# Hybrid decoder layer: weight loads ahead of the last store, five open steps, another order of the down products

## The chip, the cores and the metric

The kernel runs on one core of a Trainium2 chip. The metric is the device time of one execution in microseconds. Five engines with queues of their own work side by side: TensorE (PE, matmuls; its weight loads are listed apart as PEld), VectorE (DVE), ScalarE (ACT), GpSimd (POOL) and SyncE (SP), which here issues all DMAs. Each works through its own queue in order.

## The reference, cut to what matters

One layer over 1024 tokens of width 1024. An input projection feeds two attention groups; their outputs are mixed by `w_out`. Then, in f32:

```
x   = layer_norm(ALPHA * x + mix, ln1_g, ln1_b)
gu  = x @ w_up                                    # 1024 -> 2 * 2816
ffn = (silu(gu[:, :2816]) * gu[:, 2816:]) @ w_down
x   = layer_norm(ALPHA * x + ffn, ln2_g, ln2_b)
ple = sigmoid(x @ w_ple_gate) * (p @ w_ple)
x   = layer_norm(ALPHA * x + ple, ln3_g, ln3_b)
```

The change touches the end of the first norm, both matmuls of the feed-forward part, and the second norm.

## The kernel before

Every f32 operand of a matmul is split in two parts whose sum is the operand: a high part (ACT or POOL, `hi`) and the rest (`lo`, DVE: the operand less its high part). `mm3` then issues three matmuls: high by high, high by low, low by high. So each block of 128x128 by 512 costs three matmuls, and each operand costs a split on two engines before PE can use it. A `hi` and its `lo` of one 128x1024 operand are called a split below. The third matmul of a block needs the `lo` of the weights.

The feed-forward part multiplies two-by-two blocks with seven products in place of eight (sums and differences of blocks stand in for the eighth). Its tiles:

- **Up stage** (`u_prod`, `u_evac`): 22 steps i of 128 hidden columns. Each has seven products (i, n), n = 1 to 7, of 12 matmuls each. Products 1 and 2 need the gate weights of the step as they are ("g", L1025 or L1031, split by `u_split(i, "g")`). 5, 6, 7 and 3 need sums of weight blocks (`u_sum`, four POOL operations of 128x512, then splits "s12" and "s34"); 4 needs the split "u". On the other side stand seven operands made of the transposed first-norm output: "11" and "21" from token blocks 0 to 3; "22", "t1" to "t4" need also blocks 4 to 7 (`tr_x1` transposes a block, `t_sums` subtracts, `put` splits into place; one `put` is two small operations of 128x256 on ACT and two on DVE).
- **The order of the up products** is a list `seq`, written out before the loop: first (i,1), (i,2) of the first SKEW steps (the open steps), which need no sums and only "11" and "21"; then step by step the others. `at_pos(k, ...)` hangs fetches, sums, splits and `put`s on places k of that list. The Python order is the order in each engine's queue.
- **The end of the first norm**: for token block tb, `out_proj(tb)` multiplies by `w_out`, ACT scales, `x1_done(tb)` multiplies and adds the norm's weights on DVE (L914, L918) and stores the block to DRAM (L1190). SP's queue is in order, so what stands behind a store waits until the store's data is there.
- **Down stage**: 77 units (n, m), seven products of 11 pairs m each, in the order `ORDER` (L1225). A unit loads two 128x512 pieces into one of four staging buffers `kk` (`d_load`, four units ahead), splits them (`d_split`, two units ahead) and multiplies into four PSUM banks B. Products 1, 6, 5, 3 go to banks XB, products 2, 7, 4 to YB; 1, 2 and 7 start from fresh banks, the others go on adding in theirs. After each product DVE adds the banks to the residual `acc` (L1346 to L1352).
- **Beside the down units** the table `more` hangs work on places k: every fourth unit a weight of the last stage (`pT`, `wple`, `wgate`) is loaded and split (POOL `hi`, L107, then DVE `lo`), and from unit `base` on the second norm of blocks 0 to 3 is made in steps (`ln2_step`: statistics on DVE and POOL, scaling on ACT, weights on DVE).

Tiles named `b` come from a pool of 43 buffers of 128x1024, tiles named `h` from 12 of 128x512; PSUM has eight banks. A load into a buffer waits until its last reader is done. `hd` and `td` are DRAM tiles: hidden blocks and sums of down weights, written during the up stage and read by the down units.

Of the kernel before, what the change touches and what calls it, by code (L numbers as in the profile page):

```python
# [11 lines left out]
OP = mybir.AluOpType  # L12
# [5 lines left out]
NB = T // 128  # L18
# [16 lines left out]
SLOTS = 43  # L35
HALVES = 12
DPAIRS = 11
SKEW = 4
PVLAG = 2
CDMA = 1  # L40
LATK = (1, 1)
# [26 lines left out]
def body(tc, sb, dr, A, out, dbg, stop):  # L68
# [13 lines left out]
    def hslot(dt=F32, n=512):  # L82
        return sb.tile([128, 512], dt, name="h", tag="h", bufs=HALVES)[:, :n]
# [915 lines left out]
    def t_sums(tb):  # L999

        b11, b21, b12, b22 = TX[tb - 4, "11"], TX[tb - 4, "21"], TX.pop((tb, "12")), TX[tb, "22"]
        t2 = hslot()
        dve.tensor_sub(b11, b12, b11)
        dve.tensor_sub(t2, b22, b11)
        pool.tensor_tensor(b12, b22, b12, op=OP.subtract)
        pool.tensor_tensor(b21, b21, t2, op=OP.subtract)
        TX.update({(tb, "t1"): b11, (tb, "t2"): t2, (tb, "t3"): b12, (tb, "t4"): b21})

    def put(tb, nm):
# [149 lines left out]
    for i in range(NF):  # L1159
        s12, s34 = min(pos[i, 5], pos[i, 6]), min(pos[i, 7], pos[i, 3])  # L1160
        first = min(s12, s34)
        if i >= SKEW:
            at_pos(pos[i, 1] - 2, u_split, i, "g")
        at_pos(first - 6, u_sum, i, 0)
        at_pos(first - 5, u_sum, i, 1)
        at_pos(first - 4, u_split, i, "u")
        at_pos(s34 - 2, u_split, i, "s34")
        at_pos(s12 - 2, u_split, i, "s12")
        if i < SKEW:
            at_pos(max(first - 9, 0), u_fetch, i)  # L1170
        else:
            at_pos(min(pos[i, 1] - 2, first - 6) - 5, u_fetch, i)
        if i % 2:
            m = i // 2
            at_pos(pos[i, 4] + 2, h_sums, m)
            k = min(pos[i, 4] + 1, len(seq) - 36 + 2 * m)
            at_pos(k - 5, d_fetch, m)
            at_pos(k, d_sums, m)
    for k, nm, tbs in ((0, "t2", (6,)), (2, "t3", (4, 5)), (4, "t2", (7,)), (4, "t3", (6, 7)), (5, "t1", (4, 5, 6, 7)),
                       (7, "22", (4, 5, 6, 7)), (9, "t4", (4, 5, 6, 7))):  # L1180
        for tb in tbs:
            at_pos(k, put, tb, nm)

# [11 lines left out]
    for tb in range(NB):  # L1195
        if tb + 2 < NB:
            out_load(tb + 2)
        if tb + 1 < NB:
            out_split(tb + 1)
        if tb in (6, 7):  # L1200
            g_fetch(tb - 6)
        if tb:
            x1_done(tb - 1)
        if tb == 7:
            u_split(0, "g")
        nrm = out_proj(tb)
        if tb:
            tr_x1(tb - 1)
        act.activation(acc[tb], acc[tb], AF.Identity, scale=nrm[0], bias=nrm[1])
        if 1 <= tb <= 4:  # L1210
            put(tb - 1, "11")
            put(tb - 1, "21")
        elif tb:
            t_sums(tb - 1)
    WO = None
    put(4, "t2")
    put(5, "t2")
    if stop == 3:
# [3 lines left out]
        return  # L1222


    ORDER = (1, 2, 6, 7, 5, 3, 4)  # L1225
    units = [(n, m) for n in ORDER for m in range(DPAIRS)]
    RW, UN = {}, {}

# [18 lines left out]
    for k, (i, n) in enumerate(seq):  # L1247
        u_prod(i, n)
        if last:
            u_evac(*last)  # L1250
        if k == 0:
            u_split(1, "g")
            x1_done(NB - 1)
        elif k == 2:
            tr_x1(NB - 1)
            t_sums(NB - 1)
        if k in (1, 3):
            u_split(k // 2 + 2, "g")
        if k in (0, 2):
            g_fetch(k // 2 + 2)  # L1260
        jobs(k)
        last = i, n
        if len(seq) - 6 <= k < len(seq) - 2:
            d_load(k - len(seq) + 6)
    u_evac(*last)
    d_split(0)
    d_split(1)
    h_sums(DPAIRS - 1)
    for k in sorted(todo):
        todo[k] = [x for x in todo[k] if x[0] is not h_sums]  # L1270
# [23 lines left out]

    more = {}
    for n, it in enumerate(range(tail, len(items))):
        more[24 + 4 * n] = [(split, it + 1)]
    base = 6 * DPAIRS
    NR = {}

    def ln2_step(tb, what):
# [10 lines left out]
            norm_b(acc[tb], ln2, "d")  # L1312
    for tb in range(4):
        for what, d in ((0, 0), (1, 2), (2, 3)):
            more.setdefault(base + 2 * tb + d, []).append((ln2_step, tb, what))
    XB, YB = {}, {}
    for k, (n, m) in enumerate(units):
        if m == 0:
# [13 lines left out]
        if k in (2, 13):  # L1332
            for tb in range(k // 11 * 4, k // 11 * 4 + 4):
                acc[tb] = slot(n=D)
                nc.sync.dma_start(acc[tb], x1d[tb])
        if k == 5 * DPAIRS:
            ln2 = load_ln(2)
        for fn, *args in more.pop(k, []):
            fn(*args)
        if m == DPAIRS - 1:  # L1340
            lft, rgt = slice(0, 512), slice(512, D)
            for b in range(4):
                x, y = acc[b], acc[4 + b]
                if n in (1, 6, 5, 3):
                    o = {1: x[:, lft], 6: y[:, lft], 5: y[:, rgt], 3: x[:, rgt]}[n]
                    dve.scalar_tensor_tensor(o, o, ALPHA, B[b], op0=OP.mult, op1=OP.add)  # L1346
                elif n != 7:
                    o = {2: x[:, lft], 4: y[:, lft]}[n]
                    dve.tensor_add(o, o, B[b])
            if n == 5:  # L1350
                for b in range(4):
                    dve.tensor_add(acc[4 + b][:, rgt], acc[4 + b][:, rgt], YB[b])  # L1352
            if n == 3:
                XB = None
# [136 lines left out]
```

## Time and profile before

| | before |
|---|---|
| median of 3 runs | 1488.2 us (1487.64 to 1489.09) |
| the profiled execution | 1483.0 us, span 1481.2 us |
| mean granted clock of TensorE | 0.986 |
| PE busy | 1416.6 us (96%) |
| DVE, ACT, POOL busy | 1008.2, 710.0, 588.1 us |
| DMA | 159.33 MB, mean 108 GB/s |

The runs are timed without the profiler, the profiled execution is one more. Busy is the time in which an engine has an instruction under way; matmuls overlap, so a busy PE is not PE at its peak. Start times in rows count from the start of the span. A number in brackets behind a row of the timeline is the time for which the engine was idle before it, with the instruction that ended this.

### The profile page before, as it was taken

The numbers are of one execution on the slowest core, as the hardware profiler recorded it, in microseconds if no ns is written. First come the engines' busy times: TensorE is split into PE (matmuls) and PEld (weight loads), VectorE is DVE, ScalarE is ACT, GpSimd is POOL, SyncE is SP. The second block draws the span as 40 slices with busy tenths as digits, with TensorE's granted clock in tenths as the row PEclk, the third lists the DMA queues.
The fourth block names the chain that finished last, engine by engine and source line by source line (L and its number), as shares of the span: only waits on it lengthen the run. The fifth ranks groups of instructions, "written<-read, shape, count | busy, mean of one in ns | idle before, by whom it ended". The sixth has DMA issues, their size and how long they took to land. (4 is left out here: it accounts for less than half of the span.)

```text
span 1481.2 us, 20524 instructions
## 1 busy us (share of the span) xinstructions
PE 1416.6 (96%) x7082; PEld 1179.7 (80%) x7082; DVE 1008.2 (68%) x1921; ACT 710.0 (48%) x1447; POOL 588.1 (40%) x572
## 2 busy tenths in 40 slices
PE   8999999999989999998799999999998999998997
PEld 8987878888778887886588888888877888776886
DVE  5367599999988898676855555555543555558775
ACT  3323499888888886333523333333332433333221
POOL 1321255644533347013466666666671000012331
PEclk9999899999999999999899999999999999999999
DMA  7031000000000023223155444444636766761001
GB/s 271 15 100 51 26 1 23 1 1 15 2 15 1 1 67 133 72 99 114 56 189 176 153 152 151 146 158 157 219 137 241 275 235 220 238 211 63 29 29 57
DMA packets 66344, 159.33 MB, mean 108 GB/s; under 512 B 8000, under 2 KB 8640, under 8 KB 66240
## 3 DMA queue, kind: packets, MB, share of 16 engines
q1 hardware_dynamic: 66240, 158.02, 30.9%
q8 instruction: 56, 0.92, 0.3%
q14 instruction: 48, 0.39, 0.1%
HBM read 117.88 MB, written 40.11 MB: 107 GB/s over the span
## 5 line engine op out<-in xcount | busy, mean ns | idle before, releaser
L122 PE MATMUL p<-b 128*128 128x512 f32 (+3 forms) x1524 | 585.8, 384 | 20.7 <-ACT b L105 11.7
L123 PE MATMUL p<-b 128*128 128x512 f32 (+3 forms) x1524 | 583.8, 383 | 12.4 <-DVE b L111 12.4
L124 PE MATMUL p<-b 128*128 128x512 f32 (+3 forms) x1524 | 584.1, 383 | 5.2 <-DVE b L111 4.8
L111 DVE TENSOR_TENSOR b<-b 128x1024 fp32r<-128x1024 f32 (+4 forms) x162 | 205.8, 1289 | 239.3 <-ACT b L105 136.6
L122 PEld LDWEIGHTS p<-b 128*128 128x128 f32 x1524 | 288.6, 189 | 76.6 <-ACT b L105 13.1
L123 PEld LDWEIGHTS p<-b 128*128 128x128 f32 x1524 | 288.7, 189 | 69.8 <-DVE b L111 18.5
L124 PEld LDWEIGHTS p<-b 128*128 128x128 f32 x1524 | 288.0, 189 | 65.0 <-DVE b L111 12.1
L111 DVE TENSOR_TENSOR h<-p,h 128x512 fp32r<-128x512 f32 (+1 forms) x244 | 148.8, 628 | 11.6 <-ACT h L105 10.2
L107 POOL TENSOR_SCALAR b<-b 128x1024 fp32r<-128x1024 f32 (+3 forms) x45 | 48.4, 1081 | 254.2 <-DMA b<-in_pT 77.5
L532 ACT ACTIVATE b<-b,st 128x640 f32<-128x640 f32 (+7 forms) x192 | 142.8, 744 | 9.3 <-DVE st L481 7.0
L481 DVE CUSTOM_DVE_ANT_0 b<-s,b 128x640 f32<-128x640 f32 (+7 forms) x192 | 137.5, 716 | 10.2 <-PE s L486 6.8
L105 ACT ACTIVATE h<-p 128x512 fp32r<-128x512 f32 (+1 forms) x244 | 131.9, 551 | 25.3 <-PE p L591 22.0
L105 ACT ACTIVATE b<-kk 128x1024 fp32r<-128x1024 f32 x77 | 81.0, 1059 | 123.9 <-DMA kk<-in_wdown 56.4
L591 PE MATMUL p<-ident,b 128*128 128x128 f32 x816 | 129.4, 276 | 4.9 <-DVE b L732 1.9
L537 POOL TENSOR_SCALAR b<-b,st,gate 128x640 f32<-128x640 f32 (+7 forms) x128 | 101.0, 790 | 79.7 <-DVE st L579 40.3
L1084 ACT ACTIVATE h<-p 128x512 f32<-128x512 f32 x66 | 39.2, 594 | 183.0 <-PE p L124 176.8
L105 ACT ACTIVATE b<-b 128x1024 fp32r<-128x1024 f32 (+2 forms) x124 | 105.2, 858 | 36.9 <-POOL b L1044 14.2
L591 PEld LDWEIGHTS p<-ident,b 128*128 128x128 f32 x816 | 100.5, 142 | 24.8 <-DVE h L111 3.3
L486 PE MATMUL s<-b 128*128 128x320 f32 (+10 forms) x480 | 105.9, 341 | 3.9 <-DVE st L579 1.7
L111 DVE TENSOR_TENSOR b<-kk,b 128x1024 fp32r<-128x1024 f32 x77 | 92.9, 1248 | 23.9 <-ACT b L105 23.4
L607 PE MATMUL p<-h,b 128*128 128x512 f32 x228 | 104.1, 456 | 1.1 <-DVE h L111 0.9
L486 PEld LDWEIGHTS s<-b 96*128 96x128 f32 (+1 forms) x480 | 81.5, 192 | 21.7 <-issue 5.6
(176 smaller groups left out, 1698.9 us busy)
## 6 DMA issues: line engine op xcount, KB each, us to landing
b<-in_wup SPq DMA_DIRECT2D x48, 512.0 KB, 4.9
hd<-h SPq DMA_DIRECT2D x77, 256.0 KB, 2.2
kk<-hd SPq DMA_DIRECT2D x77, 256.0 KB, 4.6
b<-in_wdown SPq DMA_DIRECT2D x22, 512.0 KB, 4.5
td<-b SPq DMA_DIRECT2D x44, 256.0 KB, 2.7
kk<-td SPq DMA_DIRECT2D x44, 256.0 KB, 4.7
kk<-in_wdown SPq DMA_DIRECT2D x33, 256.0 KB, 5.2
b<-in_wT SPq DMA_DIRECT2D x8, 512.0 KB, 4.0
```

The lines of the kernel that those rows point to most:

```text
L105: act.activation(h, x, AF.Copy)
L107: pool.tensor_scalar(h, x, 1.0, 1.0, op0=OP.mult, op1=OP.mult)
L111: dve.tensor_sub(l, x, f(h))
L122: pe.matmul(ps, ah, bh, start=start, stop=False, skip_group_check=more)
L123: pe.matmul(ps, ah, bl, start=False, stop=False, skip_group_check=more)
L124: pe.matmul(ps, al, bh, start=False, stop=stop, skip_group_check=more)
L481: dve.tensor_tensor_reduce(out=W, in0=ps, in1=bias, op0=OP.add, op1=OP.min, scale=scale, scalar=LOWEST, accum_out=m)
L486: pe.matmul(ps, q, k[:, c0:c1], start=i == 0, stop=i == len(terms) - 1)
L532: act.activation(w, w, AF.Exp, bias=self.low[:, m:m + 1], scale=-1.0, accum_out=self.sum[:, m:m + 1])
L537: pool.tensor_scalar(w, w, self.inv[:, m:m + 1], self.gates[m], op0=OP.mult, op1=OP.mult)
L591: pe.transpose(pt[:rows, i * 128:i * 128 + 128], u.WH if col < 0 else u.W[:, col:col + rows], ident)
L607: pe.matmul(ch.bank[:, c], v, th, start=start, stop=False)
```

## The change

It does five things. SKEW goes from 4 to 5, so ten products stand ahead of the first that needs "t2". The gate weights of steps 2 and 3 and both halves of step 0's weights are loaded before the last token block's product, that is ahead of the last store in SP's queue, and the split of step 1 moves there too. For the last token block the two subtractions of `t_sums` that POOL made go to DVE, and the `put`s get other places. The splits of the first two down units move two products up, into the end of the up stage. In the down stage `ORDER` changes, the weights of the last stage are fetched four units ahead of their split, and the second norm of blocks 0 to 3 starts at unit 56 with five units per block (before: unit 66, two units per block).

```diff
@@ -35,7 +35,7 @@
 SLOTS = 43
 HALVES = 12
 DPAIRS = 11
-SKEW = 4
+SKEW = 5
 PVLAG = 2
 CDMA = 1
 LATK = (1, 1)
@@ -1000,10 +1000,11 @@
 
         b11, b21, b12, b22 = TX[tb - 4, "11"], TX[tb - 4, "21"], TX.pop((tb, "12")), TX[tb, "22"]
         t2 = hslot()
+        eng = dve if tb == NB - 1 else pool
         dve.tensor_sub(b11, b12, b11)
         dve.tensor_sub(t2, b22, b11)
-        pool.tensor_tensor(b12, b22, b12, op=OP.subtract)
-        pool.tensor_tensor(b21, b21, t2, op=OP.subtract)
+        eng.tensor_tensor(b12, b22, b12, op=OP.subtract)
+        eng.tensor_tensor(b21, b21, t2, op=OP.subtract)
         TX.update({(tb, "t1"): b11, (tb, "t2"): t2, (tb, "t3"): b12, (tb, "t4"): b21})
 
     def put(tb, nm):
@@ -1161,14 +1162,14 @@
         first = min(s12, s34)
         if i >= SKEW:
             at_pos(pos[i, 1] - 2, u_split, i, "g")
-        at_pos(first - 6, u_sum, i, 0)
-        at_pos(first - 5, u_sum, i, 1)
+        at_pos(first - 6 if i else 1, u_sum, i, 0)
+        at_pos(first - 5 if i else 1, u_sum, i, 1)
         at_pos(first - 4, u_split, i, "u")
         at_pos(s34 - 2, u_split, i, "s34")
         at_pos(s12 - 2, u_split, i, "s12")
-        if i < SKEW:
-            at_pos(max(first - 9, 0), u_fetch, i)
-        else:
+        if 0 < i < SKEW:
+            at_pos(first - 9, u_fetch, i)
+        elif i:
             at_pos(min(pos[i, 1] - 2, first - 6) - 5, u_fetch, i)
         if i % 2:
             m = i // 2
@@ -1176,8 +1177,8 @@
             k = min(pos[i, 4] + 1, len(seq) - 36 + 2 * m)
             at_pos(k - 5, d_fetch, m)
             at_pos(k, d_sums, m)
-    for k, nm, tbs in ((0, "t2", (6,)), (2, "t3", (4, 5)), (4, "t2", (7,)), (4, "t3", (6, 7)), (5, "t1", (4, 5, 6, 7)),
-                       (7, "22", (4, 5, 6, 7)), (9, "t4", (4, 5, 6, 7))):
+    for k, nm, tbs in ((0, "t2", (6,)), (0, "t3", (4, 5)), (2, "t2", (7,)), (3, "t3", (6, 7)), (4, "t1", (4, 5)),
+                       (5, "t1", (6, 7)), (7, "22", (4, 5, 6, 7)), (10, "t4", (4, 5)), (11, "t4", (6, 7))):
         for tb in tbs:
             at_pos(k, put, tb, nm)
 
@@ -1203,6 +1204,9 @@
             x1_done(tb - 1)
         if tb == 7:
             u_split(0, "g")
+            u_split(1, "g")
+            g_fetch(2)
+            g_fetch(3)
         nrm = out_proj(tb)
         if tb:
             tr_x1(tb - 1)
@@ -1213,6 +1217,7 @@
         elif tb:
             t_sums(tb - 1)
     WO = None
+    u_fetch(0)
     put(4, "t2")
     put(5, "t2")
     if stop == 3:
@@ -1222,7 +1227,7 @@
         return
 
 
-    ORDER = (1, 2, 6, 7, 5, 3, 4)
+    ORDER = (1, 2, 6, 5, 3, 7, 4)
     units = [(n, m) for n in ORDER for m in range(DPAIRS)]
     RW, UN = {}, {}
 
@@ -1249,22 +1254,21 @@
         if last:
             u_evac(*last)
         if k == 0:
-            u_split(1, "g")
             x1_done(NB - 1)
         elif k == 2:
             tr_x1(NB - 1)
             t_sums(NB - 1)
-        if k in (1, 3):
+        if k in (1, 3, 5):
             u_split(k // 2 + 2, "g")
-        if k in (0, 2):
-            g_fetch(k // 2 + 2)
+        if k == 1:
+            g_fetch(4)
         jobs(k)
         last = i, n
         if len(seq) - 6 <= k < len(seq) - 2:
             d_load(k - len(seq) + 6)
+        if k >= len(seq) - 2:
+            d_split(k - len(seq) + 2)
     u_evac(*last)
-    d_split(0)
-    d_split(1)
     h_sums(DPAIRS - 1)
     for k in sorted(todo):
         todo[k] = [x for x in todo[k] if x[0] is not h_sums]
@@ -1294,8 +1298,9 @@
 
     more = {}
     for n, it in enumerate(range(tail, len(items))):
-        more[24 + 4 * n] = [(split, it + 1)]
-    base = 6 * DPAIRS
+        more.setdefault(20 + 4 * n, []).append((fetch, it + 1))
+        more.setdefault(24 + 4 * n, []).append((split, it + 1))
+    base = 5 * DPAIRS + 1
     NR = {}
 
     def ln2_step(tb, what):
@@ -1312,7 +1317,7 @@
             norm_b(acc[tb], ln2, "d")
     for tb in range(4):
         for what, d in ((0, 0), (1, 2), (2, 3)):
-            more.setdefault(base + 2 * tb + d, []).append((ln2_step, tb, what))
+            more.setdefault(base + 5 * tb + d, []).append((ln2_step, tb, what))
     XB, YB = {}, {}
     for k, (n, m) in enumerate(units):
         if m == 0:
@@ -1333,7 +1338,7 @@
             for tb in range(k // 11 * 4, k // 11 * 4 + 4):
                 acc[tb] = slot(n=D)
                 nc.sync.dma_start(acc[tb], x1d[tb])
-        if k == 5 * DPAIRS:
+        if k == 5 * DPAIRS - 3:
             ln2 = load_ln(2)
         for fn, *args in more.pop(k, []):
             fn(*args)
@@ -1347,7 +1352,7 @@
                 elif n != 7:
                     o = {2: x[:, lft], 4: y[:, lft]}[n]
                     dve.tensor_add(o, o, B[b])
-            if n == 5:
+            if n == 7:
                 for b in range(4):
                     dve.tensor_add(acc[4 + b][:, rgt], acc[4 + b][:, rgt], YB[b])
             if n == 3:
```

How this moves instructions, at three places. First SP's queue around the store of the last token block (x1d_7282); L1025 and L1031 are loads of up weights, in the change L1026 and L1032. Before:

```order
L1190 DMA x1d_7281<-b 128x1024
L1190 DMA x1d_7282<-b 128x1024
L1025 DMA b<-in_wup 128x1024
L1031 DMA b<-in_wup 128x1024 x2
L1025 DMA b<-in_wup 128x1024
L1031 DMA b<-in_wup 128x1024 x6
```

In the change:

```order
L1191 DMA x1d_7281<-b 128x1024
L1026 DMA b<-in_wup 128x1024 x2
L1032 DMA b<-in_wup 128x1024 x2
L1191 DMA x1d_7282<-b 128x1024
L1026 DMA b<-in_wup 128x1024
L1032 DMA b<-in_wup 128x1024 x6
```

Four loads that stood behind the store stand ahead of it; the fifth step's gate weights stand behind it.

Second, DVE at the turn from the up to the down stage. L1095 to L1100 (L1096 to L1101 in the change) evacuate the last up products, `b<-kk,b` are the splits of down units. Before:

```order
L1089 TENSOR_TENSOR h<-h,p 128x512
L1095 TENSOR_TENSOR h<-h 128x512
L1099 TENSOR_TENSOR h<-h,p 128x512
L1100 TENSOR_TENSOR h<-h 128x512
L111 TENSOR_TENSOR b<-kk,b 128x1024 x13
```

In the change:

```order
L1090 TENSOR_TENSOR h<-h,p 128x512
L111 TENSOR_TENSOR b<-kk,b 128x1024
L1096 TENSOR_TENSOR h<-h 128x512
L111 TENSOR_TENSOR b<-kk,b 128x1024
L1100 TENSOR_TENSOR h<-h,p 128x512
L1101 TENSOR_TENSOR h<-h 128x512
L111 TENSOR_TENSOR b<-kk,b 128x1024 x11
```

The splits of units 0 and 1 stand one before and one between the last evacuations.

Third, DVE near the end of the down stage: L895 to L900 are the statistics of one block's second norm, L914 and L918 its weights, `b<-b` of L111 the split of a weight of the last stage. Before:

```order
L111 TENSOR_TENSOR b<-kk,b 128x1024
L914 TENSOR_TENSOR b<-b 128x1024
L918 TENSOR_TENSOR b<-b 128x1024
L111 TENSOR_TENSOR b<-kk,b 128x1024
L895 BN_STATS ls<-b 128x6 x2
L899 BN_AGGR ls<-ls 128x2
L900 TENSOR_SCALAR ls<-ls 128x1
L111 TENSOR_TENSOR b<-kk,b 128x1024
L914 TENSOR_TENSOR b<-b 128x1024
```

In the change:

```order
L895 BN_STATS ls<-b 128x6 x2
L899 BN_AGGR ls<-ls 128x2
L900 TENSOR_SCALAR ls<-ls 128x1
L111 TENSOR_TENSOR b<-kk,b 128x1024 x3
L111 TENSOR_TENSOR b<-b 128x1024
L914 TENSOR_TENSOR b<-b 128x1024
L918 TENSOR_TENSOR b<-b 128x1024
L111 TENSOR_TENSOR b<-kk,b 128x1024
L1357 TENSOR_TENSOR b<-b,p 128x512 x4
L111 TENSOR_TENSOR b<-kk,b 128x1024
```

Between two norms' statistics stood two splits of units, now there are five.

## Rows read from the trace of the kernel before

**Rows 1.** Busy time by stretches: us, then PE, PEld, DVE, ACT, POOL, PEclk (granted), DMA.

```profile
677.00:741.20 64.20, 48.08 (x179) 36.30 (x178) 48.45 (x67) 32.55 (x69) 24.72 (x18) 0.87 0.28 90
741.20:1126.00 384.80, 383.49 (x1682) 314.44 (x1681) 206.00 (x179) 124.39 (x177) 249.56 (x161) 1.00 0.47 164
1126.00:1134.40 8.40, 4.45 (x13) 3.21 (x12) 8.18 (x6) 1.85 (x2) 5.34 (x4) 0.81 0.46 174
1280.10:1356.40 76.30, 65.50 (x277) 50.82 (x276) 54.41 (x64) 25.51 (x24) 14.33 (x13) 1.00 0.56 187
```

**Rows 2.** Timeline of PE, start of the up stage: start, us, engine, line, instruction.

```profile
677.01 0.47 PE L122 MATMUL p<-b 128*128 128x512 f32 x1
...
687.95 1.06 PE L989 MATMUL p<-ident,b 128*128 128x128 f32 x8
...
741.24 0.39 PE L122 MATMUL p<-b 128*128 128x512 f32 x1
...
743.96 0.39 PE L122 MATMUL p<-b 128*128 128x512 f32 x1
```

**Rows 3.** Timeline of PE at the turn to the down stage.

```profile
1125.99 0.39 PE L122 MATMUL p<-b 128*128 128x512 f32 x1
1130.33 0.50 PE L123 MATMUL p<-b 128*128 128x512 f32 x1 [3.95 <-DVE b L111]
```

**Rows 4.** Timeline of PE in the down stage, and the transposes behind it.

```profile
1280.10 0.39 PE L122 MATMUL p<-b 128*128 128x512 f32 x1
...
1285.85 0.46 PE L122 MATMUL p<-b 128*128 128x512 f32 x1 [2.87 <-DVE b L1346]
...
1356.45 1.80 PE L1289 MATMUL p<-ident,b 128*128 128x128 f32 x15
```

**Rows 5.** Timeline of SP's queue around the last store of the first norm.

```profile
672.88 15.28 SPq L1190 DMA_DIRECT2D x1d<-b  x2
688.25 0.38 SPq L1025 DMA_DIRECT2D b<-in_wup  x1
```

**Rows 6.** Timeline of ACT: gate weights of step 2; end of the up stage.

```profile
693.67 1.06 ACT L105 ACTIVATE b<-b 128x1024 fp32r<-128x1024 f32 x1 [8.64 <-DMA b<-in_wup]
...
1121.47 0.63 ACT L1090 ACTIVATE h<-h 128x512 f32<-128x512 f32 x1 [2.84 <-DVE h L1089]
...
1123.96 3.89 ACT L105 ACTIVATE b<-kk 128x1024 fp32r<-128x1024 f32 x4
```

**Rows 7.** Timeline of DVE, start of the up stage.

```profile
669.33 2.27 DVE L914 TENSOR_TENSOR b<-b 128x1024 f32<-128x1024 f32 x1 [1.45 <-ACT b L1209]
...
694.76 1.22 DVE L111 TENSOR_TENSOR b<-b 128x1024 fp32r<-128x1024 f32 x1 [6.29 <-ACT b L105]
...
699.17 5.79 DVE L1018 TENSOR_TENSOR b<-kk,b 128x256 fp32r<-128x256 f32 x4
...
715.31 2.76 DVE L1018 TENSOR_TENSOR b<-b 128x256 fp32r<-128x256 f32 x8
...
720.31 1.23 DVE L111 TENSOR_TENSOR b<-b 128x1024 fp32r<-128x1024 f32 x1 [1.64 <-ACT b L105]
```

**Rows 8.** Timeline of PE, two of its waits in the same stretch.

```profile
694.78 0.80 PE L122 MATMUL p<-b 128*128 128x512 f32 x1 [3.02 <-ACT b L105]
...
720.33 0.79 PE L122 MATMUL p<-b 128*128 128x512 f32 x1 [6.23 <-ACT b L105]
```

**Rows 9.** Timeline of POOL, the second subtraction for token block 6.

```profile
681.69 1.30 POOL L1006 TENSOR_TENSOR b<-b,h 128x512 f32<-128x512 f32 x1
```

**Rows 10.** Timeline of SP's queue, the last store of hidden sums.

```profile
1132.57 0.32 SPq L1120 DMA_DIRECT2D hd<-h  x1
```

**Rows 11.** Waits of DVE from 1134 to 1357: in all, times, longest.

```profile
DVE b L111 <- POOL b L107: 62.7, 12, 6.2
```

**Rows 12.** Busy time in the last 11 down units, columns as in rows 1.

```profile
1325.20:1356.40 31.20, 26.36 (x110) 19.68 (x109) 27.39 (x35) 10.66 (x10) 10.14 (x9) 1.00 0.41 138
```

**Rows 13.** DMA issues: count, size, median us from issue to landing.

```profile
b<-in_wup SPq DMA_DIRECT2D x48, 512.0 KB, 4.9
```

## The prediction

> **What bounds it now.** Read first the busy table by stretches, then TensorE's own rows, then the queues of the engines that it waits for. TensorE (PE) is busy for nearly all of the span, but a mean hides where the rest lies, so the stretches come first [rows 1]: in 384.8 us of the up stage PE is busy for 383.49, while the first 64.2 us of that stage have it busy for 48.08 at a mean granted clock of 0.87, the turn to the down stage has 13 matmuls in 8.4 us at 0.81, and the last 76.3 us of the down stage have 65.50. Only there can a change of order pay.
>
> The unit of account is one product of 12 matmuls: 741.24 to 743.96 is 2.72 us when nothing waits [rows 2]. From 677.01 to 741.24 there are 14 products and eight transposes (1.06): 39.1 us of work in 64.23, **25.1 lost**. Of the 77 units of the down stage (2.72 each as well), the first starts at 1125.99, the 55th at 1280.10 and the transposes behind the last at 1356.45 [rows 3, 4]. The first loses 5.5 (13 matmuls in 8.4 us, of which 12 should take 2.72), units 2 to 54 lose 154.11 - 146.88 - 5.5 = 1.7, the last 23 lose 76.35 - 62.56 = **13.8**.
>
> **Part 1, the start of the up stage.** Why PE waits there: SP's queue issues in order, the store of block 7 waits for its norm until 688.25 (the row at 672.88 covers two stores and that wait), and the gate weights of step 2 stand behind it [rows 5]. ScalarE (ACT) gets them at 693.67, 5.4 us after their issue [rows 6], VectorE (DVE) stands idle for 6.29 us until 694.76 [rows 7], and PE waits for both until 694.78 [rows 8]. From then on DVE is late with everything: PE waits 6.23 us before (0,6) at 720.33 [rows 8].
>
> The change issues four 512 KB loads right behind the store at 672.88. At 5.4 us for a load, and a little more for the fourth, they are there by about 682. So steps 2 and 3 no longer wait for a DMA. But the same loads also let GpSimd (POOL) make its four sums for step 0 from 683 to 688, behind the two subtractions of 1.3 us, the second of which begins at 681.69 [rows 9], and this is where DVE works on the norm of block 7. What that costs is in the rows of DVE: eight small splits took 2.76 us alone and four took 5.79 with POOL busy, so 0.34 and 1.45 each; an operation of 1024 columns took 1.22 alone and 2.27 beside POOL [rows 7]. Four small splits and the two halves of the norm, 3.8 us alone, so end near 690.5, and the transposes of block 7 wait for that. PE, which now gets through three products without a stop (677.0 + 3 x 2.72 = 685.2), stands for 5.3 us.
>
> From 690.5 I walk DVE's order with these durations. Split of step 2 done at 693.7, the four subtractions of block 7 (now all on DVE, 0.7 each, beside two POOL sums) at 699.5, split of step 3 at 701.5, of step 4 at 710.4 (ACT makes its half behind a silu that waits for DVE), and the weight sums of step 0 that (0,6) needs at 720.7. Before, that last split ran from 720.31 [rows 7], so **DVE is no earlier; what is gained is that PE has two more products, (4,1) and (4,2), in front of it**: 5.4 us. PE then waits about 2.4 us before (4,1) and 4.9 before (0,6). Before, the wait that ended at 694.78 was followed by matmuls at 1.2 instead of 2.4 GHz (0.80 us for the first [rows 8]), so I leave the first products behind (0,6) slow by 2.3. (0,7), (0,5) and (1,6) follow with little wait, and the 14th product ends near 733.3 and not at 741.24: **gain 8**.
>
> Low end 3.5: only the 6.29 of idle DVE comes back, less 2.8 for the four subtractions, two of which were POOL's. High end 14.6: the same walk with POOL never in DVE's way and no slow clock, 14 products by 726.6.
>
> The Trainium skill ("SBUF — State Buffer", section "Who interferes with whom") says that a VectorE operation with two SBUF inputs and a GpSimd operation that reads SBUF exclude each other, and that the one that comes second waits for the whole instruction. By that rule the four sums may cost the norm their full 5.2 us, where my walk has 2.7, and Part 1 would gain about 5.5. The 1.45 beside 0.34 agrees with it; in the kernel before no row has four sums meet this norm.
>
> **Part 2, the turn to the down stage.** PE waited 3.95 us for DVE's split of unit 0 [rows 3], which stood in DVE's order behind the last evacuations. The splits of units 0 and 1 now stand two products earlier; ACT did the first four in a row without a wait for data, and it is free after the silu at 1121.47 [rows 6]. At 1.06 for ACT's half and 1.22 for DVE's [rows 6, 7] unit 0 is split at 1124.4, before PE needs it at 1125.99. Next late: the loads of unit 4 stand in SP's queue behind the last store of the hidden sums, which waited for POOL until 1132.57 [rows 10]; that comes about 1 us earlier, so unit 4 still waits 1 us. **Gain 4.5** of 5.5; low end 2.7, if the second split takes 2.27 for 1.22 beside POOL and half of the slow clock stays; high end 5.5.
>
> **Part 3, in the down stage.** Every fourth unit a weight of the last stage was fetched and split in one go: POOL waits for the DMA, DVE's half waits for POOL, and in DVE's queue the splits of the next units stand behind it: twelve waits, 62.7 us, the longest 6.2 [rows 11]. With four staging buffers the early ones were absorbed, the late ones not. Fetched four units (10.9 us) ahead of its split, a load of some 5 us has landed and POOL has done its half when DVE comes to it: all twelve waits go. The last 11 units have their own cause: four norms make DVE busy for 27.39 of 31.20 us [rows 12]. Spread over 20 units, at some 4.3 us each, they leave DVE 30 us of work in the 29.9 of the seventh product and less in the last, and DVE enters it one to two units ahead of PE. Of the 15.5 lost in units 2 to 77 I leave 2.5. **Gain 13.**
>
> The new order puts two products in the same banks behind one another three times (6 to 5, 5 to 3, 7 to 4) where there was one such place (5 to 3), and there PE waited 2.87 us for DVE's evacuation [rows 4]. I cost these at nothing, because that DVE was late by the wait that goes: bank 0 is complete 2.0 us before its next matmul. Low end: all three at 2.87, 15.5 - 8.6 = 6.9. High end 15.5. The earlier load of the norm's weights is two issues on SP and hidden.
>
> **Sum.** 8 + 4.5 + 13 = 25.5 us. The profiled execution took 1483.0 (its span 1481.2) and the median of the runs is 1488.2, 5.2 higher; no stretch shows where those 5.2 lie, so I take the difference alone over: 1488.2 - 25.5 = **1462.7**. All low ends give 13.1 (1475.1), all high ends 35.6 (1452.6).
>
> **Rivals.** (a) POOL takes back the start: its sums lie on DVE's path throughout, and Part 1 gives 3.5 or less. For it: four splits for 5.79. Against: the sums of step 2 now wait for a split that comes after those of step 0. 1488.2 - 21 = 1467.2. The rule of the Trainium skill quoted in Part 1 points this way. (b) The same-bank places cost what the one in the trace did: Part 3 gives 6.9, 1468.8. (c) Slower: a fifth open step and the earlier loads hold more of the 43 SBUF buffers; a load waits in SP's queue for a buffer, and all behind it waits too. It decides once a step's load comes some 14 us later than now, since a step takes 7 x 2.72 = 19 us of PE and a load 4.9 [rows 13]. If each of the 17 later steps then stalls for 3.02 us, as PE did at 694.78 [rows 8], that is 51.3, less the 25.5: 1514.0. Against: PE is idle for 1.3 us in the 384.8 of that stage [rows 1]. (d) The loads moved ahead still wait, now for buffers that PE frees late, and the splits for theirs: the change does not do what it says, within 0.2%.
>
> **Numbers.** Forecast 0.74, (a) 0.12, (b) 0.08, (c) 0.03, (d) 0.03. 0.2% is 3 us, about what a measurement of this kernel tells from no change. Faster by more 0.94, within 0.03, slower 0.03. The range 1454 to 1475 takes in the forecast with its bounds, (a) and (b).
>
> **What would show it.** Right: PE starts (1,1) and (2,1) with no DMA in any wait; a wait of some 5 us before the transposes of block 7; no wait of DVE on POOL's gate halves in the down stage; the first unit unstalled; PE idle for under 5 us from there to the transposes. Wrong: DVE's norm of block 7 done before 688 (more gain), waits of PE on evacuations at units 33, 44 and 66 (b), SP waiting long for buffers between 745 and 1126 (c).

## The result and the profile after

| | before | after |
|---|---|---|
| median of 4 runs | 1488.64 us (1487.64 to 1489.43) | 1463.97 us (1462.20 to 1465.34) |
| ratio | | 0.9834, 95% interval 0.9817 to 0.9851 |
| the profiled execution | 1483.0 us, span 1481.2 us | 1464.8 us, span 1463.0 us |
| PE, DVE, ACT, POOL busy | 1416.6, 1008.2, 710.0, 588.1 us | 1409.4, 1010.7, 709.9, 591.3 us |

The change is 24.7 us faster by the medians and 18.2 us by the two profiled executions. Both numbers are needed below: the parts can be found in the traces, and these sum to 18.2. Two executions of the kernel before, of 2983.76 and 6235.68 us beside others of 1479.7 to 1491.2, count in no median and no ratio here.

Busy time of the profile after by stretches, columns as in [rows 1]. The first answers to the first of [rows 1] (14 products), the last to [rows 12], in a window 1.2 us shorter.

```profile
677.00:734.20 57.20, 45.35 (x179) 35.95 (x178) 46.73 (x67) 30.19 (x66) 21.75 (x16) 0.88 0.29 94
734.20:1119.60 385.40, 383.63 (x1682) 314.60 (x1681) 208.84 (x182) 127.23 (x180) 252.13 (x161) 1.00 0.47 165
1119.60:1128.00 8.40, 8.40 (x39) 6.95 (x38) 6.43 (x5) 0.93 (x1) 6.41 (x4) 1.00 0.38 147
1128.00:1148.00 20.00, 14.36 (x55) 10.75 (x54) 7.27 (x6) 7.27 (x7) 0.00 (x0) 0.93 0.87 326
1308.20:1338.20 30.00, 29.97 (x132) 24.85 (x133) 23.05 (x28) 9.03 (x9) 5.59 (x5) 1.00 0.42 137
```

The 14 products take 57.2 us where they took 64.2. The turn at 1119.60 has PE busy throughout (39 matmuls in 8.4 us, before 13). The last 11 units are full (29.97 of 30.00 us). But a new hole stands from 1128 to 1148: PE has 14.36 of 20 us, with the DMA engines busy for 0.87 of the time.

PE's timeline at the start of the up stage and in the down stage, for [rows 2, 3, 4]:

```profile
691.17 1.94 PE L989 MATMUL p<-ident,b 128*128 128x128 f32 x8 [5.71 <-DVE b L918]
...
710.58 0.50 PE L122 MATMUL p<-b 128*128 128x512 f32 x1 [3.01 <-ACT b L105]
...
720.76 0.50 PE L122 MATMUL p<-b 128*128 128x512 f32 x1 [2.02 <-ACT b L105]
...
734.27 0.39 PE L122 MATMUL p<-b 128*128 128x512 f32 x1
...
1119.61 0.39 PE L122 MATMUL p<-b 128*128 128x512 f32 x1
...
1132.50 0.49 PE L122 MATMUL p<-b 128*128 128x512 f32 x1 [1.85 <-ACT b L105]
...
1144.26 0.50 PE L122 MATMUL p<-b 128*128 128x512 f32 x1 [2.27 <-ACT b L105]
...
1338.28 1.91 PE L1293 MATMUL p<-ident,b 128*128 128x128 f32 x16
```

The wait ahead of the transposes of block 7 (691.17) is there, then waits before (4,1) at 710.58 and (0,6) at 720.76; the first down unit starts at 1119.61 without a wait, and units 4 and 7 have one each. (Units are counted from 0 from here on.)

Why the norm of block 7 is late, on DVE (L1019 is L1018 of before), and POOL's first and last sum of step 0 (L1041 to L1045):

```profile
682.10 5.46 DVE L1019 TENSOR_TENSOR b<-h,b 128x256 fp32r<-128x256 f32 x4 [1.75 <-ACT b L1017]
687.49 2.28 DVE L914 TENSOR_TENSOR b<-b 128x1024 f32<-128x1024 f32 x1
689.80 1.23 DVE L918 TENSOR_TENSOR b<-b 128x1024 f32<-128x1024 f32 x1
...
720.81 1.22 DVE L111 TENSOR_TENSOR b<-b 128x1024 fp32r<-128x1024 f32 x1 [1.71 <-ACT b L105]
```

```profile
683.16 1.30 POOL L1041 TENSOR_TENSOR b<-b 128x512 f32<-128x512 f32 x1 [0.16 <-DMA b<-in_wup]
...
687.25 1.44 POOL L1045 TENSOR_TENSOR b<-b 128x512 f32<-128x512 f32 x1
```

Four operations of `put`s (128x256) take 5.46 us while POOL makes its four sums, and the norm ends at 691.0. The split that (0,6) needs runs from 720.81, before from 720.31 [rows 7].

What feeds the waits at units 4 and 7: ACT stands idle for a load of down weights, and SP's queue shows why that load is late (L1121 the last store of hidden sums, L1238 and L1243 the two loads of a unit, L1340 the loads of the first norm's rows).

```profile
1131.39 1.06 ACT L105 ACTIVATE b<-kk 128x1024 fp32r<-128x1024 f32 x1 [10.86 <-DMA kk<-in_wdown]
...
1143.15 1.06 ACT L105 ACTIVATE b<-kk 128x1024 fp32r<-128x1024 f32 x1 [6.86 <-DMA kk<-in_wdown]
```

```profile
1124.12 0.40 SPq L1119 DMA_DIRECT2D hd<-h  x1
1127.24 0.32 SPq L1121 DMA_DIRECT2D hd<-h  x1
1127.65 0.38 SPq L1238 DMA_DIRECT2D kk<-hd  x1
1128.08 0.45 SPq L1243 DMA_DIRECT2D kk<-in_wdown  x1
...
1130.52 1.96 SPq L1340 DMA_DIRECT2D b<-x1d  x4
1132.95 0.32 SPq L1238 DMA_DIRECT2D kk<-hd  x1
```

The loads of unit 4 stand behind a store that waits for POOL until 1127.24, when units 0 to 2 are nearly done; those of unit 7 stand behind four loads of 512 KB. The first of unit 7's own two loads is issued at 1132.95, long before PE needs it, and yet ACT gets the data only at 1143.15. In between the DMA engines are full, while from 1120 to 1124 they had been nearly idle (columns as in [rows 1]; the two numbers at the end are the DMA share, which can pass 1 since a packet counts where it starts, and GB/s):

```profile
1120.00:1124.00 4.00, 4.00 (x19) 3.30 (x19) 3.96 (x4) 0.53 (x1) 3.77 (x2) 1.00 0.13 50
1134.00:1144.00 10.00, 7.98 (x35) 6.25 (x34) 2.45 (x2) 2.88 (x3) 0.00 (x0) 1.00 1.04 402
```

In the rest of the down stage the waits of [rows 11] are gone but for one (DVE's waits from 1134 to 1340), and one handoff between products in the same banks is left (PE's, from 1119 to 1339):

```profile
DVE b L111 <- POOL b L107: 1.2, 1, 1.2
```

```profile
PE p L122 <- DVE b L1357: 0.6, 1, 0.6
```

The stretches of all kernels below in one table, each from the start of a matmul to the start of another in the trace, in us. With no wait, units 0 to 10 would take 11 x 2.72 = 29.9 and units 11 to 76 would take 66 x 2.72 = 179.5. The changed kernel was timed in a group of its own. The experiments were timed in three more: the parts alone with before, again; fetches alone, loads first, both and sums late; the other four. Each group has runs of the kernel before beside it, with medians of 1488.6, 1487.7, 1486.0 and 1487.7 us, so that between groups the ratio to these says more than the difference of two medians.

| kernel | median | first 14 products | rest of up stage | units 0 to 10 | units 11 to 76 | behind |
|---|---|---|---|---|---|---|
| before | 1488.64 | 64.23 | 384.75 | 35.87 | 194.58 | 124.77 |
| before, again | 1486.19 | 64.38 | 384.47 | 36.48 | 195.50 | 124.77 |
| up stage alone | 1477.65 | 57.75 | 385.17 | 36.65 | 194.91 | 124.71 |
| turn alone | 1486.67 | 64.23 | 384.67 | 35.97 | 197.49 | 124.77 |
| down stage alone | 1469.34 | 64.21 | 384.75 | 35.81 | 180.41 | 124.78 |
| fetches alone | 1468.10 | 64.30 | 384.49 | 35.77 | 179.81 | 124.78 |
| **after** | 1463.97 | 57.26 | 385.34 | 38.23 | 180.43 | 124.75 |
| after, loads first | 1462.28 | 57.08 | 385.40 | 37.23 | 180.43 | 124.75 |
| after, rows spread | 1462.32 | 57.51 | 385.22 | 35.97 | 180.67 | 124.72 |
| after, both | 1457.99 | 57.82 | 385.33 | 29.92 | 180.65 | 124.75 |
| after, both, no turn | 1462.61 | 57.85 | 385.24 | 36.58 | 180.71 | 124.72 |
| after, sums late | 1460.34 | 54.04 | 385.09 | 35.88 | 180.42 | 124.74 |
| best | 1453.40 | 54.24 | 385.32 | 29.97 | 179.82 | 124.71 |
| best, norm first | 1456.31 | 57.55 | 385.37 | 29.92 | 179.82 | 124.72 |

So the 18.2 us between the two profiles are 7.0 at the start, less 0.6 in the rest of the up stage, **less 2.4 in units 0 to 10**, and 14.1 in units 11 to 76.

### The profile page after: what moved, and what is told of

It is laid out like the page before. It is cut to its first block, busy times and chain, and to the rows that moved or that the text cites. A ratio compares the mean times of both kernels' runs of the same rounds, so it can differ in the third digit from the quotient of the medians.

```text
span 1463.0 us, 20518 instructions
## 1 busy us (share of the span) xinstructions
PE 1409.4 (96%) x7082; PEld 1179.3 (81%) x7082; DVE 1010.7 (69%) x1923; ACT 709.9 (49%) x1447; POOL 591.3 (40%) x570
## 3 DMA queue, kind: packets, MB, share of 16 engines
q1 hardware_dynamic: 66384, 158.54, 31.2%
## 5 line engine op out<-in xcount | busy, mean ns | idle before, releaser
L111 DVE TENSOR_TENSOR b<-b 128x1024 fp32r<-128x1024 f32 (+4 forms) x162 | 204.0, 1277 | 173.4 <-ACT b L105 134.4
L111 DVE TENSOR_TENSOR h<-p,h 128x512 fp32r<-128x512 f32 (+1 forms) x244 | 148.8, 627 | 12.0 <-ACT h L105 10.8
L111 DVE TENSOR_TENSOR b<-kk,b 128x1024 fp32r<-128x1024 f32 x77 | 95.5, 1262 | 48.7 <-ACT b L105 47.6
```

The costliest lines, as they stand in the source:

```text
L111: dve.tensor_sub(l, x, f(h))
```

## The experiments

### The three parts alone

**Up stage alone.** The diff without its parts in the down stage and without the earlier splits of units 0 and 1.

> The kernel before with the changes of the up stage alone (five open steps, loads and splits ahead of the last store, subtractions on DVE, places of the puts). As the two profiles have it: 6.4 us faster (PE loses 29.3 us in the up stage before and 22.9 after), with PE's 5.7 us wait ahead of the transposes of block 7 and no DMA in its waits. As predicted: 8 us faster. Rival, that the 6.5 us by which the medians differ more than the profiles lie in this stage: about 13 us faster.

Measured: ratio 0.9938 (0.9917 to 0.9959), so 9.2 us faster (6.1 to 12.3); the first 14 products 6.5 us shorter in the trace, PE's wait ahead of the transposes 5.59. The interval takes in 6.4 and 8 and leaves out 13.

**Turn alone.**

```diff
+        if k >= len(seq) - 2:
+            d_split(k - len(seq) + 2)
     u_evac(*last)
-    d_split(0)
-    d_split(1)
```

> The kernel before with the splits of the first two down units two products earlier, and nothing else. As predicted: 4.5 us faster, the first unit unstalled. Theory from the profile after: the first unit's 5.7 us go, but the loads of units 4 to 7 still stand behind the last store and beside four loads of the first norm's rows, so PE loses some 8 us in units 3 to 7 instead; between 3 us slower and no change.

Measured: ratio 0.9997 (0.9984 to 1.0009), no change that can be measured. Units 0 to 10 take 35.97 us, before 35.87: unit 0 loses nothing and units 3, 4 and 7 lose 5.8 instead. The predicted 4.5 is outside the interval.

**Down stage alone.** The new `ORDER`, the fetches four units ahead and the spread second norm.

> The kernel before with the new order of the down products, the fetches four units ahead and the spread second norm, the turn as before. As the two profiles have it: 13.7 us faster (units 2 to 77 lose 14.5 us before and 0.8 after, without units 3 to 7), with no wait of DVE for POOL's halves. As predicted: 13 us. Rival, that the handoffs between products in the same banks cost 2.9 us each where DVE is late: about 7 us.

Measured: ratio 0.9885 (0.9866 to 0.9903), 17.1 us faster (14.4 to 19.9); units 11 to 76 14.2 us shorter in the trace. The interval leaves out the rival's 7 us, and it leaves out the predicted 13 and the 13.7 of the profiles too: by the runs this part is worth more than either. One handoff costs 0.6 us (product 7 to 4, ahead of unit 66), the other two nothing.

The three medians add up to 9.2 + 0.4 + 17.1 = 26.7 us; together they give 24.7.

**Before, again**, with no edit.

> The kernel before, unchanged. Its profiled execution was 5.2 us under the median of its runs, and no stretch shows where these lie. If executions of it differ by so much, this profile is near 1488 and some stretch of it is longer than in the first profile; if a profile shortens an execution, it is near 1483 again.

Measured: profiled execution 1484.5 us, ratio 0.9988 (0.9971 to 1.0006). The nine runs go from 1479.74 to 1489.15 us, so the 1483.0 of the first profile lies within what single executions of this kernel take. Units 11 to 76 took 195.50 us in this profile and 194.58 in the first; in the two experiments above that leave that code as it was they took 194.91 and 197.49. So that stretch differs by up to 2.9 us from one execution to the next, and the profile that the prediction was read from has the shortest of the four. In the seven profiles of kernels with the new fetches and the new order of products it differs by 0.3 (180.41 to 180.71). That can be part of the 5.2 us between the first profile and its median; the rest wasn't found in any stretch and stays open.

### What of the down stage does it

**Fetches alone.** On the kernel before:

```diff
-        more[24 + 4 * n] = [(split, it + 1)]
+        more.setdefault(20 + 4 * n, []).append((fetch, it + 1))
+        more.setdefault(24 + 4 * n, []).append((split, it + 1))
```

> The kernel before with the weights of the last stage fetched four units ahead of their split, and nothing else: old order of products, second norm as before. Theory that these fetches are the down stage's loss up to its last product: DVE's waits for POOL's halves go, the single losses of 0.8 to 3.0 us at units 35 to 63 go with them (5 to 8 us), and what is left are the losses of units 67 to 76, 6.6 us in the profile before, which the four norms make: 6 to 10 us faster. Rival, that the waits were hidden by the four staging buffers and the order and the spread norm did all: under 2 us.

Measured: ratio 0.9876 (0.9859 to 0.9892), 18.4 us faster (16.0 to 21.0): all of the part's gain, and more than theory or rival had. Units 11 to 76 take 179.81 us, 0.3 over the least possible, with the old order and the four norms crowded into the last 11 units. Those units in this trace, columns as in [rows 1]:

```profile
1308.80:1340.00 31.20, 31.20 (x138) 25.50 (x137) 29.56 (x38) 11.85 (x11) 10.18 (x9) 1.00 0.40 123
```

DVE is busy for 29.56 of 31.20 us, more than the 27.39 of [rows 12], and PE doesn't wait once. So the norms alone are not the cause there. In the kernel before, DVE waited for POOL just ahead of these units and once more within them:

```profile
1320.27 1.23 DVE L111 TENSOR_TENSOR b<-b 128x1024 fp32r<-128x1024 f32 x1 [5.96 <-POOL b L107]
...
1333.47 1.22 DVE L111 TENSOR_TENSOR b<-b 128x1024 fp32r<-128x1024 f32 x1 [3.37 <-POOL b L107]
```

The second wait and the busy time make 30.8 of the 31.2 us of [rows 12]: DVE was late from these waits, and beside the norms it had no room to catch up. The handoff ahead of unit 55 that cost 2.87 us [rows 4] costs nothing here. Once the fetches are early, the new order and the spread norm add nothing; by the traces they cost 0.6 us (180.41 and 179.81), which the ratios (0.9885 and 0.9876) don't contradict. What they would be worth with the late fetches was not tried.

### The start of the up stage

**Sums late.** On the changed kernel, the loads of step 0 behind the last store:

```diff
-    u_fetch(0)
...
         if k == 0:
             x1_done(NB - 1)
+            u_fetch(0)
```

> The changed kernel with the two loads of step 0 issued behind the last store, so that POOL makes the four sums of step 0 some 10 us later and not beside DVE's last norm. If POOL's sums are what holds that norm: the four small puts ahead of it take under 2.5 us instead of 5.46, the wait ahead of the transposes of block 7 falls from 5.7 to under 3 us. What comes of it is open: the sums then run beside other puts of DVE. If all is moved: no change in time; if DVE has room there: 2 to 4 us faster. Rival, that the norm is late by DVE's own order: the wait stays at 5.7.

Measured: 1460.34 us (1459.37 to 1460.82), ratio to before 0.9823 (0.9808 to 0.9838). That is 1.6 us under the changed kernel by the ratios, whose intervals overlap, so the gain in time is shown by the trace and not by the runs: the first 14 products take 3.2 us less. DVE and PE in its trace:

```profile
682.42 2.18 DVE L1019 TENSOR_TENSOR b<-h,b 128x256 fp32r<-128x256 f32 x4 [1.75 <-ACT b L1017]
684.52 1.21 DVE L914 TENSOR_TENSOR b<-b 128x1024 f32<-128x1024 f32 x1
685.77 1.23 DVE L918 TENSOR_TENSOR b<-b 128x1024 f32<-128x1024 f32 x1
```

```profile
687.14 1.06 PE L989 MATMUL p<-ident,b 128*128 128x128 f32 x8 [1.37 <-DVE b L918]
```

DVE's order is the same, row for row. The puts take 2.18 for 5.46 us and the norm's first half 1.21 for 2.28: **POOL's four sums held this norm by 4.3 us**, and the wait falls from 5.71 to 1.37. The loads of step 0 were not what held it: in the changed kernel they had landed when the sums began at 683.16. Part of it comes back later, since the sums now meet other work of DVE: PE loses 4.5 us ahead of (4,1), 3.2 in the changed kernel. Units 0 to 10 were shorter too in this profile (35.88 and 38.23 us), with the same loads in the same places; why is not shown.

**Norm first.** On the best version below, DVE's norm of block 7 ahead of the four small puts:

```diff
-    put(4, "t2")
-    put(5, "t2")
...
             u_fetch(0)
+            put(4, "t2")
+            put(5, "t2")
```

> The version before, and on DVE the norm of block 7 ahead of the four small puts for blocks 4 and 5 that stood before it. If the norm's place on DVE is what PE waits for: no wait ahead of the transposes, up to 1.5 us faster. Rival, that DVE is the bound of the whole start: PE waits later for as much, no change.

Measured: 1456.31 us (1455.02 to 1456.53), 2.9 us slower than the best version (same group, no run in common), which neither theory nor rival had. The wait ahead of the transposes is gone, but the norm's end releases the store, the store the loads of step 0 and these POOL's sums. They begin at 693.14 where they began at 694.61, and that is 1.5 us too early for DVE's two subtractions, which had just got through in the best version (first fence); here (second fence) they take 1.78 us each:

```profile
693.28 0.69 DVE L1006 TENSOR_TENSOR kk<-kk 128x512 f32<-128x512 f32 x1
693.88 0.68 DVE L1007 TENSOR_TENSOR b<-b,h 128x512 f32<-128x512 f32 x1
694.49 1.86 DVE L1019 TENSOR_TENSOR b<-h,b 128x256 fp32r<-128x256 f32 x2
696.27 2.29 DVE L111 TENSOR_TENSOR b<-b 128x1024 fp32r<-128x1024 f32 x1
```

```profile
693.26 1.78 DVE L1006 TENSOR_TENSOR kk<-kk 128x512 f32<-128x512 f32 x1
694.96 1.77 DVE L1007 TENSOR_TENSOR b<-b,h 128x512 f32<-128x512 f32 x1
696.66 2.88 DVE L1019 TENSOR_TENSOR b<-h,b 128x256 fp32r<-128x256 f32 x2
699.46 2.28 DVE L111 TENSOR_TENSOR b<-b 128x1024 fp32r<-128x1024 f32 x1
```

The split behind them runs 3.2 us later, and PE waits 5.47 us for it until 701.79 (1.80 in the best version). This undoes the gain of the late sums: the first 14 products take 57.55 us again, for 54.24.

### The turn

All four on the changed kernel. **Loads first**: units 4 and 5 are loaded ahead of the last stores.

```diff
+    for k in (4, 5):
+        d_load(k)
     u_evac(*last)
     h_sums(DPAIRS - 1)
...
-        d_load(k + 4)
+        if k > 1:
+            d_load(k + 4)
```

> The changed kernel with the loads of units 4 and 5 issued ahead of the last stores of the hidden sums. Theory that units 3 to 7 wait because these loads stand behind a store that waits for POOL: the 3.2 us at units 3 and 4 go, those at units 6 and 7 (5.1 us), which wait beside the four loads of the norm's rows, partly stay; 3 to 6 us faster than the changed kernel. Rival, that the DMA engines are full there whatever the order: the same loss at other units, no change.

Measured: 1462.28 us, ratio 0.9839 (0.9823 to 0.9855): no difference from the changed kernel that the intervals show. Units 3 and 4 lose nothing, units 6 and 7 lose 7.3 us. PE's waits there are 4.0 us in all; the stretch from 1140 to 1150 has a mean granted clock of 0.66.

**Rows spread**: the first norm's rows are loaded one at a time.

```diff
-        if k in (2, 13):
-            for tb in range(k // 11 * 4, k // 11 * 4 + 4):
-                acc[tb] = slot(n=D)
-                nc.sync.dma_start(acc[tb], x1d[tb])
+        if k in (6, 7, 8, 9, 13, 14, 15, 16):
+            tb = k - 6 if k < 10 else k - 9
+            acc[tb] = slot(n=D)
+            nc.sync.dma_start(acc[tb], x1d[tb])
```

> The changed kernel with the four loads of the first norm's rows spread over units 6 to 9 and 13 to 16, and the loads of units 4 and 5 where they were. Theory that both causes add: units 3 and 4 lose 3.2 us as in the changed kernel, units 6 and 7 nothing; about 5 us faster than the changed kernel. Rival, that the norm's rows are the whole cause: no loss in units 0 to 10, 8 us faster.

Measured: 1462.32 us, ratio 0.9832 (0.9818 to 0.9847): again no clear difference. Units 6 and 7 lose nothing, as the theory had it; units 3 to 5 lose 6.0 us and not 3.2. Their waits are 2.6 us as in the changed kernel, but here the mean granted clock is 0.66 from 1130 to 1140 (0.50, the lower level of 1.2 GHz, from 1134 to 1138), where the changed kernel kept 1.00 until 1142. First this kernel, then the changed one:

```profile
1130.00:1140.00 10.00, 7.42 (x20) 5.18 (x19) 5.21 (x5) 5.29 (x5) 0.00 (x0) 0.66 0.85 294
```

```profile
1130.00:1142.00 12.00, 9.37 (x39) 6.87 (x37) 3.68 (x3) 3.18 (x3) 0.00 (x0) 1.00 0.97 366
```

**Both**: loads first and rows spread.

> As the one before, and the four loads of the first norm's rows one at a time at units 6 to 9 and 13 to 16 instead of four at unit 2 and four at unit 13. Theory: no unit from 0 to 10 waits for a load, 8.3 us faster than the changed kernel, near 1456. Rival, DMA bandwidth: still over 4 us lost in units 0 to 10.

Measured: 1457.99 us (1457.36 to 1458.51), ratio 0.9808 (0.9790 to 0.9826); 4.3 us under loads first, which was timed in the same group, with no run in common, and 3.9 under the changed kernel by the ratios. The theory's 8.3 us is what the traces have: units 0 to 10 take 29.92 us, the least possible, for 38.23. The runs show about half of it. From 1119 to 1150, the changed kernel and then this one:

```profile
1119.00:1150.00 31.00, 25.36 (x102) 19.79 (x101) 15.64 (x13) 9.99 (x10) 7.01 (x4) 0.94 0.72 265
```

```profile
1119.00:1150.00 31.00, 31.00 (x139) 25.66 (x138) 21.14 (x18) 13.23 (x13) 6.55 (x4) 1.00 0.88 310
```

More is moved in the same time (310 and 265 GB/s) and PE waits for none of it, so over the whole stretch bandwidth wasn't the bound. What held PE was what is issued when: the loads of unit 4 too late, while the DMA engines had next to nothing to do, and 2 MB of rows just ahead of the loads of unit 7, with which the engines were then full for 10 us. Each cause alone was enough for a stall, which is why taking away one gave almost nothing.

**Both, no turn**: as this, but the splits of units 0 and 1 again behind the last evacuations, and the two loads behind them.

> The version with spread loads, but the splits of units 0 and 1 again behind the last evacuations. Whether moving them is worth anything once the loads are out of the way: by the prediction's term the first unit loses 5.5 us again, 4.5 to 5.7 us slower than the version with spread loads. Rival, that these splits then run as early as the evacuations allow anyway: no difference.

Measured: 1462.61 us, ratio 0.9831 (0.9815 to 0.9848), 4.6 us slower than with them by the medians and 3.4 by the ratios, of two groups. Unit 0 loses 6.5 us again, and units 0 to 10 are 6.7 us longer in the trace:

```profile
1125.88 0.80 PE L123 MATMUL p<-b 128*128 128x512 f32 x1 [3.94 <-DVE b L111]
```

So the earlier splits are worth 3.4 to 6.7 us, which takes in the predicted 4.5, but only when the loads behind them are in time. In the kernel before, the 5.7 us that PE lost at unit 0 (3.95 of them a wait, the rest at the lower clock, 0.50 from 1132 to 1134) were the time in which those loads arrived.

### All together

**Best**: rows spread, loads first, sums late as above, and the old order and old places of the norm.

```diff
-    ORDER = (1, 2, 6, 5, 3, 7, 4)
+    ORDER = (1, 2, 6, 7, 5, 3, 4)
...
-    base = 5 * DPAIRS + 1
+    base = 6 * DPAIRS
...
-            more.setdefault(base + 5 * tb + d, []).append((ln2_step, tb, what))
+            more.setdefault(base + 2 * tb + d, []).append((ln2_step, tb, what))
```

> The changed kernel with spread loads and with the loads of step 0 behind the last store, and with the old order of the down products and the old places of the second norm. The fetches alone made units 11 to 76 free of waits, so the order and the spread norm should be worth nothing, and cost the 0.8 us at unit 65. Sum from the profiles: 1463.0 less 8.3 in units 0 to 10, less 3.2 in the first 14 products, less 0.6: a span of 1451, a time near 1452.5. Rival, that the order and the spread norm carry part of Part 3 beside the other changes: losses in units 66 to 76, 1456 or more.

Measured: 1453.40 us (1452.74 to 1453.73), ratio 0.9772 (0.9758 to 0.9787), span 1451.3; 9.2 us faster than the changed kernel by the ratios. The sum held, part by part: 54.24, 29.97 and 179.82 us. The runs before beside it spread over 3.6 us (1485.52 to 1489.11), its own over 1.0.

## Why the prediction was right, and where it was not

1462.7 was predicted and 1463.97 measured, inside the range and in the forecast's case. But that it came so near is in part luck: of its three terms one held, one is absent and one is larger than written. By the parts alone they are 9.2, 0.4 and 17.1 us for 8, 4.5 and 13, so that the second is 4.1 too high and the third 4.1 too low.

- **What bounds the kernel**: right. All that was gained lies in the three stretches named, and the rest of the up stage [rows 1] stayed as it was but for 0.6 us (384.75 and 385.34).
- **Part 1, 8 us**: held. 7.0 in the trace, 9.2 (6.1 to 12.3) as the part alone. The walk along DVE's order held too: norm of block 7 at 691.0 (690.5 predicted), wait ahead of the transposes 5.71 (5.3), the split for (0,6) no earlier than before (720.81 and 720.31), the 14th product done at 734.27 (733.3). Its two later waits were 3.0 and 2.0 us, not 2.4 and 4.9; with the slow clock between them the four products from (3,2) on lost 10.5, against 9.6 in the walk. That the norm's end came out to 0.5 us is luck too, for three sizes in it were off. The walk gives 3.8 us of work alone and 2.7 for POOL before 690.5, so it starts at 684.0; the row starts at 682.10. Without the sums this work takes 4.6 us and not 3.8, and POOL's sums add 4.3 and not 2.7. The Trainium skill ("SBUF — State Buffer", section "Who interferes with whom") has the second operation wait for the whole instruction of the first, and 5.2 was worked out from it. The rows lie nearer to the rule than to the walk: four small puts in 5.46 us beside four sums, in 2.18 without them. Part 1 as a whole, 7.0 us, lies between the 8 of the walk and the 5.5 by the rule.
- **Part 2, 4.5 us**: failed at the step "unit 4 still waits 1 us". The first unit is unstalled as predicted, but units 3 to 7 lose 8.3 us, so that units 0 to 10 are 2.4 us longer than before. Units 3 and 4 lose 3.2 in place of the 1, and units 6 and 7 lose 5.1 that the step didn't have: it looked at the store ahead of unit 4 and not at what else stands in SP's queue, the four loads of the first norm's rows ahead of unit 7, which keep the DMA engines full from 1134 to 1144. The stall that was removed had been the cover of both.
- **Part 3, 13 us**: the size was near in the trace (14.1) and too low by the runs of the part alone (17.1, with 14.4 to 19.9), and the mechanism half right. All twelve waits went but one of 1.2 us. The step "the last 11 units have their own cause: four norms" was wrong: the fetches alone gave 18.4 us with the norms where they were. DVE's 27.39 busy of 31.20 us were read as the cause, and they were only the reason why DVE couldn't make up for a delay that came from its waits for POOL.
- **Rival (a)**, POOL taking back the start: its mechanism is real, its price was within Part 1. **Rival (b)**: 0.6 us at one of the three handoffs, nothing at the other two; that the earlier 2.87 us hung on DVE's delay held. **Rival (c)**: a sign, but no price. SP's waits at its loads of up weights rise from 20.4 us (longest 2.4) to 40.3 (longest 7.4) in the rest of the up stage, and PE is still busy for 383.63 of 385.40 us there. **Rival (d)**: no sign.
- **The sum**: by the two profiles the change is worth 18.2 us and not 25.5. The sum was taken off a median 5.2 us above that profile, and the kernel after has no such gap (1464.8 profiled, 1463.97 median). So the difference that "no stretch shows" was not a constant that stays, and taking it over helped the prediction by luck. A part of it may lie in units 11 to 76, in the waits that the change removes (194.58 to 197.49 us in four profiles); where the rest lies wasn't settled. The stated range, too, is not quite what it says: its lower end, 1454, is above the 1452.6 of all high ends.
- **What would show it**: three of five came as written; one wait of DVE for POOL of 1.2 us was left where none was to be, and "PE idle for under 5 us" from the first unit to the transposes failed (6.2 us of waits, 9.1 lost).

## What to carry to other kernels

A stall often covers the next one in the queue: before one counts its removal as a gain, follow what its time had let arrive, load by load, behind it in the DMA queue. Where two causes each suffice for a stall, taking one away shows nothing, and both have to go in one experiment before either is called harmless. And an engine that is nearly full late in a stage is not by that the cause of waits there: look first for what made it late.

## What was not expected of the hardware

- A wait of the same length had very different prices. In the changed kernel 2.6 us of waits between 1130 and 1134 left the granted clock at 1.00 until 1142; with rows spread, 2.6 us of waits in the same place went with a mean of 0.66 from 1130 to 1140, and the units lost 6.0 us instead of 3.2. What decides between the two was not tried.
- VectorE and GpSimd fall into step: in the changed kernel four operations of 128x256 on VectorE take 5.46 us from 682.10, beside GpSimd's sums of 1.30 to 1.44 us each from 683.16 to 688.7. Three of the four take about 1.5 us each there and 0.41 with the sums late; the first takes 1.18 in both kernels, beside GpSimd's last subtraction. A start 1.5 us earlier of these sums cost the best version 2.9 us.
- The runs of a kernel may lie closer together once PE waits nowhere in units 0 to 10: 1.0 to 1.5 us apart over four runs each of the three such versions, 1.4 to 4.2 over four each of the others. Four runs say little, and why was not tried.
